# Row maxima of a two-branch attention reduced straight from PSUM, and written by one transpose and small DMAs

## The chip, the cores and the metric

One core of a Trainium2 chip runs the kernel. The metric is the device time in microseconds (us) of one execution; less is better. The core has five engines with queues of their own: TensorE (PE, matmuls), VectorE (DVE), ScalarE (ACT), GpSimd (POOL) and SyncE (SP, which only issues DMAs). Each works through its instructions in order, and waits for others by semaphores. DMAs can be issued from SP, ACT and POOL. PSUM is where matmuls write; SBUF holds everything else.

## The reference

A layer with two attentions side by side on 2048 latent tokens (a grid of 32 rows by 64 columns) and 256 context tokens, in float32. All of it is computed; the change is in how the softmax of both branches is kept from overflow.

```
# branch A: multi-head latent attention, 8 heads, 96 = 64 + 32 (rotary) dimensions
sc = einsum('bqhd,bkhd->bhqk', q, k) * scale        # 2048 queries x 2304 keys
p  = softmax(sc, axis=-1)
o  = einsum('bhqk,bkhd->bqhd', p, v)
# branch B: neighbourhood attention, 8 heads of 64, a window of 8 x 16 grid cells
s_win = einsum('bwhd,brwchd->bhwrc', qr, k_win) * scale + bias
s_ctx = einsum('bwhd,blhd->bhwl', qr, kc) * scale
p = softmax(concatenate([s_win, s_ctx], axis=-1), axis=-1)
```

Before it stand norms and one input projection, behind it gates and an output projection.

## The kernel before

The kernel runs in stages: modulation and norms (to about 200 us), the input projection (to 860), preparation for the attention (to about 1095, with the first maxima), the attention (to 2290) and the output (to 2650). Only the attention is touched.

**Branch A** is a loop over 32 units, 8 heads of 4 blocks of 512 queries. A unit has nine steps (`kp`) of 256 keys. A step computes two score tiles S (128 keys by 512 queries, three matmuls each: high and low parts of q and k), takes the exponential on ACT, adds the exponentials on POOL (`za`, L1272 and L1274) and, in bursts, multiplies them with v into `oacc` (L1224). The keys lie on the partitions of S, so the maximum of a query cannot be taken there. It is taken one unit earlier: `max_tasks(u, qh)` computes the transposed products `pm` (128 queries by up to 512 keys, L810), takes the maxima over the keys and writes their negatives into row 96 of `qh`, the high part of the next unit's queries. Row 96 of `Kh` is all ones, so the first of S's three matmuls (97 rows) subtracts the maximum.

For one tile of 128 queries the 2304 keys make five products. Two pairs of 512: the first of a pair is copied to SBUF on ACT (`msb`, L816), the second is scanned against the copy on DVE (L818), which leaves the running maximum in the last column. The rest of 256 is reduced (L823) and joined with the scan's result (L824). After four tiles, `fin` turns the four columns of `m1` into a row by four matmuls against the identity (`pmf`, L833), one row of 128 each, and ACT copies the row into `qh` (L834).

**Branch B** is a stream, `natten`, whose pieces are put between the steps of branch A by weights: `feed` hands out as many pieces as the share of steps that have passed. Per head it has 24 pieces of `n_max` for the next head (products `nm` and `nc`, reduced on DVE by L886 and L897), 24 scores `ns` (L923, L924, L940, L941) that read `KA`, `QQ`, `KBt` and `QLt`, and four pieces `fin(rb)` of `n_max`: 16 matmuls `nf` (L905) that turn the 16 columns of negated maxima into rows, and four DVE casts (L907) that write them into row 64 of `QLt`. `n_load(h)` issues the head's loads of KA, QQ, KBt, QLt, bias and v on SP's queue. It is called when the last score of the head before has been issued, and `fin` follows it.

**What sets the order.** All of it is written once in Python order and then ordered by a scheduler, which places each engine's instructions by priority and its own estimate of the time. The tasks of `max_tasks` are released by `more(frac)`: after a fraction of step `kp`, `len(tasks) * (kp + frac) / (NKP - 0.7) + 1` of them have been issued, NKP being 9. PSUM gives three buffers to `psM` and two to `psS`; `pm`, `nm`, `nc`, `ns`, S and the row matmuls take turns in these five.

Of the kernel before, what the change touches and what calls it, by code (L numbers as in the profile page):

```python
# [57 lines left out]
PB = 8  # L58
ZDVE = {1: tuple(range(1, 9))}
# [5 lines left out]
def tile_hybrid_layer(ctx: ExitStack, tc: tile.TileContext, I: dict, out: bass.AP, dbg=None):  # L65
# [81 lines left out]
    # ------------------------------------------------------------------ modulation, norms, low-rank columns  # L147
# [404 lines left out]
    # ------------------------------------------------------------------ wide columns of the in-projection  # L552
# [193 lines left out]
    # ------------------------------------------------------------------ attention  # L746
# [55 lines left out]
    def max_tasks(u, qh):  # L802
        i = (u // NB) % 2
        m1 = mq.tile([P, 4], F32, tag="m1", name=f"m1{u}")
        last = [None] * 4

        def product(qt, ci):
            a, b = ci * W, min(NK, (ci + 1) * W)
            pm = psm(f"pm{u}_{qt}_{ci}")
            nc.tensor.matmul(pm[:, :b - a], qh[0:DK, qt * P:(qt + 1) * P], Kh[i][0:DK, a:b], start=True, stop=True)  # L810
            return pm

        def pair(qt, ci):
            p0 = product(qt, ci)
            sb = mq.tile([P, W], F32, tag="msb", name=f"msb{u}_{qt}_{ci}")
            nc.scalar.activation(sb, p0, AF.Copy)  # L816
            p1 = product(qt, ci + 1)
            nc.vector.tensor_tensor_scan(sb, p1, sb, -3.0e38 if ci == 0 else last[qt], op0=ALU.max, op1=ALU.max)  # L818
            last[qt] = sb[:, W - 1:W]

        def rest(qt):
            p0 = product(qt, 4)
            nc.vector.tensor_reduce(m1[:, qt:qt + 1], p0[:, :NK - 4 * W], axis=AX.X, op=ALU.max, negate=True)  # L823
            nc.vector.scalar_tensor_tensor(out=m1[:, qt:qt + 1], in0=last[qt], scalar=-1.0, in1=m1[:, qt:qt + 1],  # L824
                                           op0=ALU.mult, op1=ALU.min)

        def fin():
            for f in zdefer:
                f()
            zdefer.clear()  # L830
            pm = psm(f"pmf{u}")
            for t in range(4):
                nc.tensor.matmul(pm[DK:DK + 1, t * P:(t + 1) * P], m1[:, t:t + 1], ident, start=True, stop=True)  # L833
            nc.scalar.activation(qh[DK:DK + 1, :], pm[DK:DK + 1, :], AF.Copy)  # L834

        o = []
        for qt in range(4):
            o += [lambda q=qt: pair(q, 0), lambda q=qt: pair(q, 2), lambda q=qt: rest(q)]
        return o + [fin]

    # neighbourhood stream
    def grid(ap):
        return ap.rearrange("p (r c) -> p r c", c=GW)
# [27 lines left out]
    def n_max(h, bn):  # L871
        mx = nv.tile([P, 2, 16], F32, tag="nmx", name=f"nmx{h}")
        m1 = nv.tile([P, 16], F32, tag="nm1", name=f"nm1{h}")
        kg = grid(NKm[:, 0:S])
# [24 lines left out]
        def fin(rb):  # L899
            if rb == 0:  # L900
                nc.vector.tensor_tensor(m1, mx[:, 0, :], mx[:, 1, :], op=ALU.max)
                nc.vector.tensor_scalar_mul(m1, m1, -1.0)
            pm = psm(f"nf{h}_{rb}")
            for cb in range(4):
                nc.tensor.matmul(pm[64:65, cb * P:(cb + 1) * P], m1[:, rb * 4 + cb:rb * 4 + cb + 1], ident,  # L905
                                 start=True, stop=True)
            nc.vector.tensor_copy(rowcol(QLt[64:65, rb * W:(rb + 1) * W]), blk(pm[64:65, :]))  # L907
# [4 lines left out]
        return o + [lambda r=r: fin(r) for r in range(4)]  # L912
# [102 lines left out]
    n_weight = 24 * WM + H * (24 * WT + 24 * WM + 4 * WM + WI)  # L1015
# [3 lines left out]
    def natten(bn, d):  # L1019
        prev = None  # L1020
        mt = n_max(0, bn)
        for f in mt[:24]:
            f()
            yield WM
        if H > 1:
            bn = n_load_max(1)
        for h in range(H):
            for i, f in enumerate(mt[24:]):
                f()
                if i == 1 and prev is not None:  # L1030
                    n_store(prev)
                    n_z(prev)
                yield WM
# [3 lines left out]
            mq_ = list(mt[:24])  # L1037
# [5 lines left out]
            for pi, pr in enumerate(npairs):  # L1043
                pts = []
                for t in pr:
                    pts.append(n_score(d, t))
                    yield WT
                    nt_ += 1
                    while mq_ and 24 - len(mq_) < nt_ * 24 / 18:
                        mq_.pop(0)()  # L1050
                        if not mq_ and h + 2 < H:
                            bn = n_load_max(h + 2)
                        yield WM
                queue.append((d, pr, pts, pi == len(npairs) - 1))
                if len(queue) > 1:
                    held.append(queue.pop(0))
                    while len(held) > HELD:
                        n_pv(*held.pop(0))
# [13 lines left out]
    # output-phase weights, prepared under the last units  # L1072
# [60 lines left out]
    # prologue  # L1133
# [100 lines left out]
    for u in range(nu):  # L1234
# [15 lines left out]
        for kp in range(NKP):  # L1250
            pt = mp.tile([P, 2, W], F32, tag="P", name=f"P{u}_{kp}", bufs=PB)
            def more(frac):
                nonlocal done
                want = min(len(tasks), int(len(tasks) * (kp + frac) / (NKP - 0.7) + 1))
# [42 lines left out]
    # ------------------------------------------------------------------ output  # L1297
# [231 lines left out]
```

## Time and profile before

| | us |
|---|---|
| three runs | 2643.67, 2647.04, 2649.07 |
| median | 2647.04 |
| span of the profiled execution | 2650.0 |
| PE busy (98% of the span) | 2588.5 |
| DVE busy (47%) | 1256.2 |
| ACT busy (39%) | 1037.3 |
| POOL busy (39%) | 1031.0 |
| mean granted clock of PE | 0.995 of 2.4 GHz |

The profiled execution has no time of its own beside its span of 2650.0 us, which is 3.0 us above the median of the three runs. Busy time is the union of an engine's records; PE's records overlap, since the next matmul begins while the one before still drains, so the cost of a matmul is read from the distance between starts and not from the length of its record.

### The profile page before, as it was taken

Reading aid. Unit: us, or ns where it says so; the run is one execution under the profiler, and the core shown is the slowest. Engines: PE = TensorE matmul, PEld = TensorE weight load, DVE = VectorE, ACT = ScalarE, POOL = GpSimd, SP = SyncE. Lnnn points to the kernel's source line nnn. Section 1 sums busy time; section 2 is a strip of 40 time slices with the busy share of each in tenths; the row PEclk is TensorE's granted clock in tenths of the full one; section 3 lists DMA queues with packets and bytes.
Section 4 is the critical chain, followed back from the end, with each engine's and each line's share of the span. In section 5 each row is a group of like instructions: output and inputs, shape, how many; then the busy total and the mean of one; then the engine's idle time right before and its main releaser. Section 6 shows DMA issues by size and latency. Waiting matters only on the chain.

```text
span 2650.0 us, 36033 instructions
## 1 busy us (share of the span) xinstructions
PE 2588.5 (98%) x13244; PEld 1861.2 (70%) x13244; DVE 1256.2 (47%) x2132; ACT 1037.3 (39%) x2030; POOL 1031.0 (39%) x797
## 2 busy tenths in 40 slices
PE   7999999999999999999999999999999999999998
PEld 4778888877799788555555656555555564798998
DVE  4663221223200310665665757574756557465564
ACT  4663332222211221455544545554545555222221
POOL 1211111112300000566665757676767686232220
PEclk9999999999999999999999999999999999999999
DMA  7536765456634465605041231414131305765552
GB/s 257 192 91 183 261 205 177 141 174 194 188 107 127 152 213 165 162 17 126 9 108 50 57 80 37 116 37 106 35 91 43 79 23 181 229 192 175 164 164 68
DMA packets 182985, 342.94 MB, mean 129 GB/s; under 512 B 25130, under 2 KB 95950, under 8 KB 175438
## 3 DMA queue, kind: packets, MB, share of 16 engines
q1 hardware_dynamic: 168872, 299.01, 38.0%
q0 software_dynamic: 13504, 41.35, 5.5%
q8 instruction: 104, 1.70, 0.3%
q14 instruction: 73, 0.60, 0.1%
q10 hardware_dynamic: 432, 0.28, 0.0%
HBM read 214.42 MB, written 126.13 MB: 129 GB/s over the span
## 4 chain that ended last, share of the span: by engine, by line
PE 87%; DVE 8%; issue 2%; DMA 1%; ACT 1%; SPq 0%; POOL 0%; DVEq 0%; ACTq 0%; POOLq 0%
PE accm L135 24%; PE S L1264 13%; PE oacc L1224 11%; PE ya L135 6%; PE pm L810 6%; PE f L135 5%; PE vacc L135 4%; DVE msb L818 3%; PE nacc L226 3%; PE no L980 3%; DVE m L824 2%; PE accf L135 2%; PE accx L135 1%; PE nf L905 1%; PE pstl L185 1%
## 5 line engine op out<-in xcount | busy, mean ns | idle before, releaser
L1274 POOL TENSOR_TENSOR za<-za,P 128x1024 f32<-128x1024 f32 x217 | 515.4, 2375 | 217.2 <-ACT P L1266 214.5
L1266 ACT ACTIVATE P<-S 128x512 f32<-128x512 f32 x576 | 340.4, 595 | 246.8 <-PE S L1264 237.2
L135 PE MATMUL accm<-hh,whi 128*128 128x512 f32 x928 | 367.0, 395 | 0.0
L135 PE MATMUL accm<-hl,whi 128*128 128x512 f32 x928 | 366.9, 395 | 0.0
L135 PE MATMUL accm<-hh,wlo 128*128 128x512 f32 x928 | 366.7, 395 | 0.0
L1224 PE MATMUL oacc<-P,V 128*64 128x512 f32 x1152 | 318.7, 615 | 0.0
L1264 PE MATMUL S<-qh,Kh 97*128 97x512 f32 x576 | 240.5, 418 | 7.7 <-DVE msb L818 3.0
L818 DVE TENSOR_TENSOR_SCAN msb<-pm,msb 128x512 f32<-128x512 f32 x128 | 155.8, 1218 | 162.8 <-ACT msb L816 137.3
L1264 PE MATMUL S<-ql,Kh 96*128 96x512 f32 x576 | 229.7, 399 | 0.0
L1264 PE MATMUL S<-qh,Kl 96*128 96x512 f32 x576 | 228.3, 396 | 0.0
L810 PE MATMUL pm<-Kh,qh 96*128 96x512 f32 (+1 forms) x640 | 215.0, 399 | 5.5 <-DVE msb L818 3.9
L816 ACT ACTIVATE msb<-pm 128x512 f32<-128x512 f32 x256 | 151.9, 594 | 167.0 <-PE pm L810 160.3
L818 DVE TENSOR_TENSOR_SCAN msb<-pm,msb,msb 128x512 f32<-128x512 f32 x128 | 163.8, 1280 | 95.5 <-ACT msb L816 93.8
L135 PEld LDWEIGHTS accm<-hh,whi 128*128 128x128 f32 x928 | 174.3, 188 | 42.6 <-issue 0.8
L135 PEld LDWEIGHTS accm<-hh,wlo 128*128 128x128 f32 x928 | 174.3, 188 | 41.9
L135 PEld LDWEIGHTS accm<-hl,whi 128*128 128x128 f32 x928 | 174.3, 188 | 41.8 <-issue 0.4
L810 PEld LDWEIGHTS pm<-Kh,qh 96*128 96x128 f32 x640 | 110.8, 188 | 116.7 <-issue 43.0
L135 PE MATMUL ya<-u,woh 128*128 128x256 f32 x1024 | 185.0, 284 | 0.2
L1224 PEld LDWEIGHTS oacc<-P,V 128*64 128x64 f32 x1152 | 73.5, 137 | 137.2 <-issue 133.9
L135 PE MATMUL f<-wfh,y 128*128 128x512 f32 (+1 forms) x528 | 162.8, 387 | 2.9 <-ACT y L1334 2.1
L824 DVE SCALAR_TENSOR_TENSOR m<-msb,m 128x1 f32<-128x1 f32 x128 | 161.5, 1262 | 2.1
L135 PEld LDWEIGHTS ya<-u,woh 128*128 128x128 f32 x1024 | 160.2, 192 | 1.4 <-DVE t L1331 0.6
(1929 smaller groups left out, 4631.6 us busy)
## 6 DMA issues: line engine op xcount, KB each, us to landing
rawc<-in_wch SPq DMA_DIRECT2D x30, 512.0 KB
KA<-kB SPq DMA_DIRECT2D x16, 576.0 KB
xl<-in_xb SPq DMA_DIRECT2D x32, 256.0 KB
wm<-in_wmodb SPq DMA_DIRECT2D x8, 1024.0 KB
kmS<-sk POOLq DMA_DIRECT2D x32, 256.0 KB, 3.8
qR<-q SPq DMA_DIRECT2D x16, 512.0 KB
qm<-sq POOLq DMA_DIRECT2D x32, 256.0 KB, 3.9
woS<-ps SPq DMA_DIRECT2D x16, 512.0 KB
```

Source lines behind the costliest of these rows:

```text
L135: nc.tensor.matmul(acc, a, b, start=(i == 0), stop=(i == n - 1))
L185: nc.tensor.matmul(pst[32 * j:32 * j + 32, :w], ones[:, 0:32], sq[:, :w], start=(kt < 4), stop=(kt >= 4))
L226: nc.tensor.matmul(acc[:, :n], a[:, k, sl], b[:, k, :n], start=(k == 0 and q == 0), stop=(k == KT - 1 and q == 2))
L810: nc.tensor.matmul(pm[:, :b - a], qh[0:DK, qt * P:(qt + 1) * P], Kh[i][0:DK, a:b], start=True, stop=True)
L816: nc.scalar.activation(sb, p0, AF.Copy)
L818: nc.vector.tensor_tensor_scan(sb, p1, sb, -3.0e38 if ci == 0 else last[qt], op0=ALU.max, op1=ALU.max)
L824: nc.vector.scalar_tensor_tensor(out=m1[:, qt:qt + 1], in0=last[qt], scalar=-1.0, in1=m1[:, qt:qt + 1], op0=ALU.mult, op1=ALU.min)
L980: nc.tensor.matmul(o_, v_, p_, start=st_, stop=last and k == n - 1, skip_group_check=True)
L1224: nc.tensor.matmul(acc[x * DV:(x + 1) * DV, :], vt[:, 2 * k + x, :], p_[:, x, :], start=(k == 0), stop=(k == NKP - 1), skip_group_check=True)
L1264: nc.tensor.matmul(sp, a[0:e, ks], b[0:e, :], start=(n == 0), stop=(n == 2))
L1266: nc.scalar.activation(pt[:, x, :], sp, AF.Exp)
L1274: ve.tensor_tensor(za, za, pt, op=ALU.add)
```

## The change

`max_tasks` has 20 tasks `part` instead of twelve: each product, of 512 or 256 keys, is reduced by DVE straight from PSUM into one of 20 columns `m5`. `fin` reduces `m5` to four negated columns, turns them by one PE transpose (128x4 to 4x128), copies that with ACT to `mr`, and writes its four rows into row 96 of `qh` by four DMAs on ACT's queue. The copies `msb`, the scans and L824 are gone. In `n_max` one reduce joins and negates both halves, one transpose (`turn`, now the 25th piece taken ahead with the other 24) gives 16 rows, ACT copies them, and `fin` writes them into row 64 of `QLt` by 16 DMAs on SP's queue. `fin` is one piece in the stream where there were four, and the stores of the head before (`n_store`, `n_z`) follow it. MLEAD is 2.0 where 0.7 stood. A few comment lines are gone as well.

```diff
+MLEAD = 2.0
 ...
     def max_tasks(u, qh):
         i = (u // NB) % 2
+        m5 = mq.tile([P, 4, 5], F32, tag="m5", name=f"m5{u}")
         m1 = mq.tile([P, 4], F32, tag="m1", name=f"m1{u}")
-        last = [None] * 4
-
-        def product(qt, ci):
+        mr = mq.tile([4, P], F32R, tag="mr", name=f"mr{u}")
+
+        def part(qt, ci):
             a, b = ci * W, min(NK, (ci + 1) * W)
             pm = psm(f"pm{u}_{qt}_{ci}")
             nc.tensor.matmul(pm[:, :b - a], qh[0:DK, qt * P:(qt + 1) * P], Kh[i][0:DK, a:b], start=True, stop=True)
-            return pm
-
-        def pair(qt, ci):
-            p0 = product(qt, ci)
-            sb = mq.tile([P, W], F32, tag="msb", name=f"msb{u}_{qt}_{ci}")
-            nc.scalar.activation(sb, p0, AF.Copy)
-            p1 = product(qt, ci + 1)
-            nc.vector.tensor_tensor_scan(sb, p1, sb, -3.0e38 if ci == 0 else last[qt], op0=ALU.max, op1=ALU.max)
-            last[qt] = sb[:, W - 1:W]
-
-        def rest(qt):
-            p0 = product(qt, 4)
-            nc.vector.tensor_reduce(m1[:, qt:qt + 1], p0[:, :NK - 4 * W], axis=AX.X, op=ALU.max, negate=True)
-            nc.vector.scalar_tensor_tensor(out=m1[:, qt:qt + 1], in0=last[qt], scalar=-1.0, in1=m1[:, qt:qt + 1],
-                                           op0=ALU.mult, op1=ALU.min)
+            nc.vector.reduce_max(m5[:, qt, ci:ci + 1], pm[:, :b - a], axis=AX.X)
 ...
             zdefer.clear()
+            nc.vector.tensor_reduce(m1, m5, axis=AX.X, op=ALU.max, negate=True)
             pm = psm(f"pmf{u}")
+            nc.tensor.transpose(pm[0:4, 0:P], m1, ident)
+            nc.scalar.activation(mr, pm[0:4, 0:P], AF.Copy)
             for t in range(4):
-                nc.tensor.matmul(pm[DK:DK + 1, t * P:(t + 1) * P], m1[:, t:t + 1], ident, start=True, stop=True)
-            nc.scalar.activation(qh[DK:DK + 1, :], pm[DK:DK + 1, :], AF.Copy)
+                nc.scalar.dma_start(bc(qh[DK:DK + 1, t * P:(t + 1) * P]), bc(mr[t:t + 1, :]))
 ...
-        def fin(rb):
-            if rb == 0:
-                nc.vector.tensor_tensor(m1, mx[:, 0, :], mx[:, 1, :], op=ALU.max)
-                nc.vector.tensor_scalar_mul(m1, m1, -1.0)
-            pm = psm(f"nf{h}_{rb}")
-            for cb in range(4):
-                nc.tensor.matmul(pm[64:65, cb * P:(cb + 1) * P], m1[:, rb * 4 + cb:rb * 4 + cb + 1], ident,
-                                 start=True, stop=True)
-            nc.vector.tensor_copy(rowcol(QLt[64:65, rb * W:(rb + 1) * W]), blk(pm[64:65, :]))
+        def turn():
+            nc.vector.tensor_reduce(m1, mx.rearrange("p t q -> p q t"), axis=AX.X, op=ALU.max, negate=True)
+            pm = psm(f"nf{h}")
+            nc.tensor.transpose(pm[0:16, 0:P], m1, ident)
+            nc.scalar.activation(mr, pm[0:16, 0:P], AF.Copy)
+
+        def fin():
+            for qb in range(16):
+                rb, cb = divmod(qb, 4)
+                nc.sync.dma_start(grid(bc(QLt[64:65, :]))[:, rb * 8:rb * 8 + 8, cb * 16:cb * 16 + 16],
+                                  bc(mr[qb:qb + 1, :]).rearrange("o (r c) -> o r c", r=8))
 ...
-    n_weight = 24 * WM + H * (24 * WT + 24 * WM + 4 * WM + WI)
+    n_weight = 25 * WM + H * (24 * WT + 25 * WM + WM + WI)
 ...
-            for i, f in enumerate(mt[24:]):
+            for i, f in enumerate(mt[25:]):
                 f()
-                if i == 1 and prev is not None:
+                if prev is not None:
 ...
-                want = min(len(tasks), int(len(tasks) * (kp + frac) / (NKP - 0.7) + 1))
+                want = min(len(tasks), int(len(tasks) * (kp + frac) / (NKP - MLEAD) + 1))
```

How the change moves instructions is shown at three places. The first is PE at the end of unit 13, where unit 14's maxima are finished. `pm14_3_4` is the last product of unit 14, `S13_8_1` the second score tile of unit 13's last step, `zp12` belongs to unit 12's sums, `ns3` and `nc4` to the heads 3 and 4 of branch B; the last column is the output's shape, and the number at the end of a name only tells buffers apart. Before:

```order
L810 MATMUL pm14_3_4_12868<-Kh1_8343,qh14_12288 128x256
L895 MATMUL nc4_4_12873<-NKm_8336,NQs_8337 128x256 x2
L1264 MATMUL S13_8_0_12878<-qh13_11953,Kh1_8343 128x512
L1264 MATMUL S13_8_0_12878<-ql13_12339,Kh1_8343 128x512
L1264 MATMUL S13_8_0_12878<-qh13_11953,Kl1_8345 128x512
L1180 MATMUL zp12_12883<-za12_12292,ones_68 32x128 x4
L833 MATMUL pmf14_12891<-ident_63,m114_12606 1x128 x3
L940 MATMUL ns3_('w', 3, 1)_12897<-QQ_8341,KA_8339 128x352
L833 MATMUL pmf14_12891<-ident_63,m114_12606 1x128
L941 MATMUL ns3_('w', 3, 1)_12897<-QLt_8338,KBt_8340 128x352
L1264 MATMUL S13_8_1_12904<-qh13_11953,Kh1_8343 128x512
L1264 MATMUL S13_8_1_12904<-ql13_12339,Kh1_8343 128x512
```

After, with lines 10 lower:

```order
L812 MATMUL pm14_3_4_12719<-Kh1_8343,qh14_12174 128x256
L1254 MATMUL S13_7_0_12723<-qh13_11847,Kh1_8343 128x512
L1254 MATMUL S13_7_0_12723<-ql13_12221,Kh1_8343 128x512
L1254 MATMUL S13_7_0_12723<-qh13_11847,Kl1_8345 128x512
L1170 MATMUL zp12_12728<-za12_12180,ones_68 32x128 x4
L821 MATMUL pmf14_12737<-ident_63,m114_12487 4x128
L883 MATMUL nc4_4_12744<-NKm_8336,NQs_8337 128x256 x2
L1254 MATMUL S13_7_1_12748<-qh13_11847,Kh1_8343 128x512
L1254 MATMUL S13_7_1_12748<-ql13_12221,Kh1_8343 128x512
L1254 MATMUL S13_7_1_12748<-qh13_11847,Kl1_8345 128x512
L871 MATMUL nm4_10_12754<-NKm_8336,NQs_8337 128x480
L930 MATMUL ns3_('w', 3, 1)_12758<-QQ_8341,KA_8339 128x352
```

Before, the first score of unit 14, `S14_0_0`, follows this piece after the rest of `S13_8_1`, two pairs of `oacc`, two `no` and one `nm`. Now the single transpose stands ahead of `S13_7_1`, and up to `S14_0_0` come the rest of `ns3`, the two tiles of step 8, two pairs of `oacc` and one `nm`.

The second place is ACT, the same end of unit 13. `P13_7` and `P13_8` are exponentials of steps 7 and 8. Before:

```order
L1266 ACTIVATE P13_7_12850<-S13_7_1_12863 128x512
L944 ACTIVATE np3_('w', 0, 1)_12857<-np3_('w', 0, 1)_12857 128x384
L1266 ACTIVATE P13_8_12877<-S13_8_0_12878 128x512
L1183 ACTIVATE zs12_12888<-zp12_12883 128x128
L834 ACTIVATE qh14_12288<-pmf14_12891 1x512
L944 ACTIVATE np3_('w', 3, 1)_12898<-np3_('w', 3, 1)_12898 128x352
L1266 ACTIVATE P13_8_12877<-S13_8_1_12904 128x512
```

After, where the four rows of `mr14` go to `qh14` by DMA:

```order
L1256 ACTIVATE P13_7_12722<-S13_7_0_12723 128x512
L1173 ACTIVATE zs12_12733<-zp12_12728 128x128
L822 ACTIVATE mr14_12488<-pmf14_12737 4x128
L824 DMA qh14_12174<-mr14_12488 1x16x8 x4
L1256 ACTIVATE P13_7_12722<-S13_7_1_12748 128x512
L934 ACTIVATE np3_('w', 3, 1)_12759<-np3_('w', 3, 1)_12759 128x352
L1256 ACTIVATE P13_8_12765<-S13_8_0_12766 128x512
```

One copy has become one smaller copy and four DMA issues, which stand a step earlier, ahead of the exponential of `S13_7_1`.

The third place is SP's queue at head 1, where its loads are issued. Before:

```order
L792 DMA V_10663<-vaS 128x1152
L857 DMA KA<-kB_119 64x2304
L858 DMA KA<-kB_119 64x2304
L859 DMA QQ<-qR_123 64x2048
L860 DMA QQ<-qR_123 64x2048
L861 DMA KBt<-kB_119 64x2304
L862 DMA QLt<-qR_123 64x2048
L864 DMA bt_9969<-in_biasT 128x480
L1193 DMA zmS_106<-zs_9992 4x128
```

After, with ten rows of `nmr` (the sixteen turned maxima) ahead of the loads and six behind them:

```order
L896 DMA QLt<-nmr_8903 1x8x16 x10
L793 DMA V_10596<-vaS 128x1152
L844 DMA KA<-kB_119 64x2304
L845 DMA KA<-kB_119 64x2304
L1183 DMA zmS_106<-zs_9914 4x128
L846 DMA QQ<-qR_123 64x2048
L847 DMA QQ<-qR_123 64x2048
L848 DMA KBt<-kB_119 64x2304
L849 DMA QLt<-qR_123 64x2048
L851 DMA bt_9945<-in_biasT 128x480
L777 DMA qh_9963<-qm_77 96x512
L896 DMA QLt<-nmr_8903 1x8x16 x6
```

The loads stand in the same order; what is new are the sixteen small DMAs around them.

## Rows read from the trace of the kernel before

**Rows 1.** Busy us (records) by engine in the attention, granted clock, DMA share, GB/s:

```profile
860.00:2260.00 1400.00, 1364.18 (x6505) 840.73 (x6504) 783.94 (x1101) 659.88 (x1198) 794.92 (x445) 0.99 0.34 90
```

**Rows 2.** PE's waits, 860 to 2290 us: us in total, times, longest:

```profile
PE pmf L833 <- DVE m L824: 14.8, 17, 3.4
PE pm L810 <- DVE msb L818: 3.9, 14, 0.4
PE S L1264 <- DVE msb L818: 3.0, 9, 0.6
```

**Rows 3.** Groups of PE by form, 860 to 2290 us: records, busy us, mean ns:

```profile
L833 PE MATMUL pmf<-ident,m 128*1 128x128 f32 x256 | 36.6, 273 | 15.0 <-DVE m L824 14.8
L905 PE MATMUL nf<-ident,nm 128*1 128x128 f32 x256 | 32.5, 272 | 0.0
```

**Rows 4.** Timeline of PE from 1113 us: start, duration, line, operation, records:

```profile
1113.10 1.03 PE L905 MATMUL nf<-ident,nm 128*1 128x128 f32 x8
1114.07 0.50 PE L1264 MATMUL S<-qh,Kh 97*128 97x512 f32 x1
...
1114.96 1.03 PE L905 MATMUL nf<-ident,nm 128*1 128x128 f32 x8
1115.93 1.07 PE L1224 MATMUL oacc<-P,V 128*64 128x512 f32 x2
1116.93 0.51 PE L810 MATMUL pm<-Kh,qh 96*128 96x512 f32 x1
```

**Rows 5.** Groups of DVE by form in the attention:

```profile
L818 DVE TENSOR_TENSOR_SCAN msb<-pm,msb,msb 128x512 f32<-128x512 f32 x128 | 163.8, 1280 | 95.5 <-ACT msb L816 93.8 <-PE ns_('w', 2, 2)_13301 L941 0.3
L824 DVE SCALAR_TENSOR_TENSOR m<-msb,m 128x1 f32<-128x1 f32 x128 | 161.5, 1262 | 2.1
L818 DVE TENSOR_TENSOR_SCAN msb<-pm,msb 128x512 f32<-128x512 f32 x128 | 155.8, 1218 | 162.8 <-ACT msb L816 137.3 <-PE S L1264 20.3 <-PE pm L810 4.4
L823 DVE TENSOR_REDUCE m<-pm 128x1 f32<-128x256 f32 x128 | 53.2, 415 | 23.8 <-PE pm L810 22.4
L897 DVE TENSOR_REDUCE nmx<-nc 128x2 f32<-128x512 f32 x64 | 43.6, 682 | 41.5 <-PE nc L895 41.5
```

**Rows 6.** Timeline of all engines at the end of unit 13:

```profile
1604.63 2.35 POOL L1274 TENSOR_TENSOR za<-za,P 128x1024 f32<-128x1024 f32 x1 [1.78 <-ACT P L1266]
...
1605.29 1.71 DVE L824 SCALAR_TENSOR_TENSOR m<-msb,m 128x1 f32<-128x1 f32 x1
...
1607.06 0.38 PE L833 MATMUL pmf<-ident,m 128*1 128x128 f32 x2 [0.42 <-DVE m L824]
...
1607.47 0.59 ACT L834 ACTIVATE qh<-pmf 1x512 fp32r<-1x512 f32 x1 [1.34 <-PE pmf L833]
...
1611.49 0.40 PE L1264 MATMUL S<-qh,Kh 97*128 97x512 f32 x1
```

**Rows 7.** Groups of ACT by form in the attention:

```profile
L816 ACT ACTIVATE msb<-pm 128x512 f32<-128x512 f32 x256 | 151.9, 594 | 167.0 <-PE pm L810 160.3 <-DVE msb L818 6.0
...
L1183 ACT ACTIVATE zs<-zp 128x128 f32<-128x128 f32 x30 | 8.2, 272 | 0.8 <-PE zp L1180 0.8
```

**Rows 8.** The tile zmS, a 2 KB DMA per unit: issue to landing:

```profile
DMA to landing us min/median/max: 1.9/2.0/2.0
```

**Rows 9.** Timeline of SP's queue at head 1: start, duration of the issue:

```profile
1228.42 0.45 SPq L857 DMA_DIRECT2D KA<-kB  x1
1228.91 0.59 SPq L858 DMA_DIRECT2D KA<-kB  x1
...
1231.46 0.59 SPq L862 DMA_DIRECT2D QLt<-qR  x1
```

**Rows 10.** Timeline of PE at head 1:

```profile
1228.23 0.33 PE L941 MATMUL ns_('w', 2, 3)_9867<-QLt,KBt 113*128 113x360 f32 x1
...
1258.12 0.40 PE L923 MATMUL ns_('c', 0, 0)_10104<-QQ,KA 128*128 128x512 f32 x1
```

**Rows 11.** Busy us and DMA in the window of head 1's loads:

```profile
1228.00:1258.00 30.00, 30.00 (x177) 17.14 (x177) 12.95 (x18) 14.19 (x26) 17.29 (x9) 1.00 0.68 156
```

More of the change, by code (lines that the diff above doesn't have):

```diff
@@ L830, in fin @@
             zdefer.clear()
+            nc.vector.tensor_reduce(m1, m5, axis=AX.X, op=ALU.max, negate=True)
             pm = psm(f"pmf{u}")
+            nc.tensor.transpose(pm[0:4, 0:P], m1, ident)
+            nc.scalar.activation(mr, pm[0:4, 0:P], AF.Copy)
             for t in range(4):
-                nc.tensor.matmul(pm[DK:DK + 1, t * P:(t + 1) * P], m1[:, t:t + 1], ident, start=True, stop=True)
-            nc.scalar.activation(qh[DK:DK + 1, :], pm[DK:DK + 1, :], AF.Copy)
[L836 to L839, printed above, removed]
+                nc.scalar.dma_start(bc(qh[DK:DK + 1, t * P:(t + 1) * P]), bc(mr[t:t + 1, :]))
+        return [lambda q=qt, c=ci: part(q, c) for qt in range(4) for ci in range(5)] + [fin]
     def grid(ap):
@@ L873, in n_max @@
         m1 = nv.tile([P, 16], F32, tag="nm1", name=f"nm1{h}")
+        mr = nv.tile([16, P], F32R, tag="nmr", name=f"nmr{h}")
         kg = grid(NKm[:, 0:S])
@@ L911, in n_max @@
             o += [lambda q=2 * b2: win(q), lambda q=2 * b2 + 1: win(q), lambda b=b2: cmax(b)]
-        return o + [lambda r=r: fin(r) for r in range(4)]
+        return o + [turn, fin]
     def n_score(d, t):
@@ L1021, in natten @@
         mt = n_max(0, bn)
-        for f in mt[:24]:
+        for f in mt[:25]:
             f()
@@ L1036, in natten @@
                 mt = n_max(h + 1, bn)
-            mq_ = list(mt[:24])
+            mq_ = list(mt[:25])
             d["za"] = nv.tile([P, S], F32, tag="nza", name=f"nza{h}")
@@ L1048, in natten @@
                     nt_ += 1
-                    while mq_ and 24 - len(mq_) < nt_ * 24 / 18:
+                    while mq_ and 25 - len(mq_) < nt_ * 25 / 18:
                         mq_.pop(0)()
```

## The prediction

> **What bounds the kernel now.** First the table of stretches, to see which engine is full where the change acts. In the attention (860 to 2260 us) PE is busy 1364.18 of 1400 us at a granted clock of 0.99 of 2.4 GHz; DVE has 783.94, ACT 659.88 and POOL 794.92 [rows 1]. So PE is the bound: a matmul taken away there is worth its whole time, a DVE or ACT instruction is worth only the PE wait that it causes, and 35.8 us of PE idle is all that waits can give. The second view is PE's list of waits. Its three largest entries are the row matmuls pmf behind L824 (14.8 us in 17 waits), the products pm behind the scan L818 (3.9) and the scores S behind the same scan (3.0), 21.7 us together [rows 2]. All three go back to the chain that the change replaces. No load stands in that list.
>
> **Removed: row matmuls on PE.** Each record of pmf and nf reads 272 or 273 ns and there are 256 of each [rows 3], but records overlap, so I take a spacing. Eight nf records are four matmuls (two records for one fp32 matmul): they begin at 1113.10 and the next matmul at 1114.07, 0.97 us, so one costs 0.2425 us [rows 4]. Before there are 32x4 pmf and 8x16 nf matmuls; after, one transpose of the same 128 moving columns per unit and per head. 32x3 + 8x15 = 216 matmuls go: 216 x 0.2425 = **52.4 us**, on the path. Nothing hides it: at the row matmuls PE is the busy engine. The transpose has four or sixteen stationary columns where a row matmul has one, a form that no row shows. If it took twice the 0.2425, the 40 would cost 10 us more; if nothing, 10 us less. I take 0.2425, the row with the same moving operand.
>
> **Replaced: the maxima.** For one query tile DVE now does 1.218 (scan), 1.280 (scan), 0.415 (reduce of 256) and 1.262 (L824, on one element a row), 4.2 us, 16.7 us per unit [rows 5]. After: sixteen reduces of 512 from PSUM at 0.682 (the reduce L897 reads the same shape) and four at 0.415 make 12.6 us, and a last reduce of 4x5 numbers. That last one has no row. At least it costs the accumulator read of about 0.1, at most the 1.262 of L824; I take 0.4 us, near L823. DVE is under no pressure either way: four us per unit less is worth nothing by itself. On ACT 256 copies of 0.594 us (151.9) and the copies L834 go [rows 7]; ACT was not the bound, so this is worth nothing by itself either.
>
> What it can give is PE's waits. L824 is the case: its shortest work is tiny, yet it takes 1.262 on the mean. At the end of unit 13 it starts at 1605.29 and ends at 1607.00, and the POOL addition that started at 1604.63 ends at 1606.98; PE then starts the last pmf at 1607.06 after a wait of 0.42 us [rows 6]. The two-input DVE instruction ends when the POOL one does. The Trainium skill ("SBUF — State Buffer", section "Who interferes with whom") says that a DVE instruction with two SBUF inputs contends with a GpSimd instruction that reads SBUF, and that `tensor_reduce` on trn2 never contends; the row on L824 agrees with the first half, and no row of before shows the second, a reduce from SBUF beside POOL. By that rule the new last reduce is never held; without it the sum would carry up to 1.3 us per unit at this place, the rival "the waits stay". With no copy before the scan, a product is free for reuse after one reduce instead of ACT and then a scan, so the waits of pm and S should go too. The transpose still waits for the last pm, its reduce (0.415) and the small reduce; between the last pm and pmf the order above shows one S score (three matmuls) and the zp matmuls, about 1.2 us. I let 18 of the 21.7 us go and keep about 4.
>
> **Added: the row by DMA, per unit.** Before, ACT writes row 96 of qh straight from PSUM: at unit 13's end from 1607.47 for 0.59 us, and S of unit 14 starts at 1611.49, 3.4 us after it [rows 6]. After, the way is: ACT copy of 4x128 (nearest row zs, 272 ns [rows 7]), four DMA issues on ACT's queue, and a landing. An issue is priced by SP's of 0.45 to 0.59 us [rows 9], since no row shows one on ACT beside activations; a 2 KB transfer of the same kind, zmS, lands 1.9 to 2.0 us after its issue [rows 8]. With about 0.3 for the two handovers: 0.3 + 0.27 + 4x0.52 + 2.0 = 4.65 us; at least 4.4 and, with ACT busy in an exponential of 0.6, 5.3. The cover is PE's work between pmf and S. MLEAD 2.0 sets fin one step earlier, so that three scores of three matmuls, two pairs of oacc and six smaller matmuls stand there at unit 14. A score takes 0.89 (1114.07 to 1114.96) and a pair 1.00 (1115.93 to 1116.93) [rows 4]; the small ones, with 256 to 480 columns, some 0.15 to 0.2 each: 2.7 + 2.0 + 1.1 = 5.8 us, 5.0 where scores follow each other closely. So it is mostly hidden, narrowly: cover less chain lies between -0.3 and 1.4 at a typical unit, and a few units have a score less between. I charge 0.5 us to each of 32 units, **+16**; the ends are 0 and 1.5 (0 to 48). Behind the four issues on ACT stand the exponentials of the next score tile; they come 2 us later and are needed only two steps on, by oacc, so I add nothing.
>
> The Trainium skill ("DMA: Bandwidth & Descriptors", "Rules for kernel authors") speaks against this: many small transfers should be coalesced into one, and under 64 KB one pays mostly overhead, of which the page's fixed part is about 2.0 us per DMA. The 1.9 to 2.0 of zmS agrees [rows 8]; if these fixed parts ran one after another instead of overlapped, the time would be that of the first rival.
>
> **Added: QLt's row, per head.** Sixteen DMAs stand on SP's queue: ten ahead of the loads of KA, QQ, KBt and QLt and six behind them (order above). The ten wait for the last read of the old QLt, as KA waits for the last read of KA. Head 1 before: last read 1228.23, KA issued 1228.42, QLt 1231.46, first score of the head 1258.12 [rows 9, 10]. That is 29.6 us in which 3.5 MB must land, while the core moves 156 GB/s on the mean at a DMA share of 0.68 [rows 11]; at full share that is 156/0.68 = 229 GB/s, 15 us, at the mean rate 22. After, the sixteen nf matmuls and two of the stream's four steps are gone from this window, and counted by the spacings the first score comes 19 to 21 us after the last read and the first read of QLt 24 to 28 us. KA now leaves 10x0.52 = 5 us later. KA and QQ (2.2 MB, 9.5 to 14 us) then land at about 17 to 21 us, all four with KBt and QLt at 22 to 29. Cover and need are about equal; the stall lies between 0 and 7 us. I take 2 us for each of 7 heads, **+14**. SP itself is mostly idle, so its other issues lose nothing.
>
> **Sum** against the profiled execution, 2650.0 us: 2650.0 - 52.4 - 18 + 16 + 14 = 2609.6. The median of the runs is 2647.04, 3.0 less, so the forecast is **2607 us**.
>
> **Rivals.** (1) **The row chain outlasts its cover.** If the four landings come one after another, the chain is 0.57 + 4x2.0 = 8.6 against a cover of 5.4: 3.2 us per unit, 32 x 3.2 = 102 in place of 16, 2693 us, slower than before. It decides from (2655 - 2593.6)/32 = 1.9 us per unit. Against it: the issues do not wait for one another's data. For: the cover is narrow. (2) **The head's loads come late.** 7 us for each of 7 heads, 49 in place of 14: 2642, no change. For it: the shorter window and five us of row DMAs ahead of KA. Against: the share of 0.68 shows room. (3) **The waits stay.** The last reduce comes behind others in DVE's order or is held like L824: 18 us are not saved, 2625. (4) **All covers hold.** No stall at units and heads and no wait left: 2650 - 52.4 - 21.7 - 3 = 2573. (5) The change does not do what it says: not so, since the 216 matmuls, the copies and the scans are gone from the built order.
>
> **Chances.** Forecast 0.48, (3) 0.18, (4) 0.15, (1) 0.10, (2) 0.09. About 0.2% (5.3 us) is what a measurement of this kernel can tell from no change. Faster by more than that: the forecast, (3), (4) and a third of (2), 0.84; within: 0.06, the rest of (2); slower: 0.10, (1). The range leaves out (1) and little of (4)'s lower end: 2572 to 2645.
>
> **What would show it.** Right: PE's records of pmf and nf fall from 512 to 80, the spacing of a transpose is 0.24; PE's list has no wait on L824 or a scan, and the last reduce takes well under 1.26; S of a new unit waits for the DMA of qh by under 1 us, ns of a new head for KA or QLt by a few. Wrong: an entry "S behind DMA qh" of 60 us or more (1), "ns behind DMA" of 50 (2), "pmf behind DVE" at 15 again (3), or a PE idle in the attention that has grown though no wait names a DMA, which I have no term for.

## The result and the profile after

| | before | after |
|---|---|---|
| median of the runs, us | 2648.06 | 2661.64 |
| range, us | 2643.67 to 2649.47 | 2653.05 to 2666.67 |
| span of the profiled execution, us | 2650.0 | 2651.2 |

The ratio after/before is 1.0054, with a 95% interval of 1.0037 to 1.0071. The change makes the kernel slower by half a per cent, where 1.5% faster was forecast. The profiled execution of after is the fastest of its four, so its trace shows some 9 us less loss than the median has.

The table of stretches, for the attention, against [rows 1]:

```profile
860.00:2260.00 1400.00, 1363.62 (x6011) 818.85 (x6010) 617.01 (x1218) 504.41 (x948) 794.35 (x445) 0.98 0.34 90
```

DVE lost 167 us and ACT 155, as the edit says. PE lost 494 records and is as busy as before: 1363.62 against 1364.18 us. That is the riddle. PE's groups, 860 to 2350 us, after:

```profile
L1214 PE MATMUL oacc<-P,V 128*64 128x512 f32 x1152 | 364.9, 620 | 1.6 <-ACT P L1256 1.5
...
L821 PE MATMUL pmf<-ident,m 128*4 128x128 f32 x32 | 8.7, 271 | 0.0
L890 PE MATMUL nf<-ident,nm 128*16 128x128 f32 x8 | 2.2, 275 | 0.0
```

and of before, the row that the prediction did not look at:

```profile
L1224 PE MATMUL oacc<-P,V 128*64 128x512 f32 x1152 | 318.7, 615 | 0.0
```

The row matmuls went from 36.6 + 32.5 [rows 3] to 8.7 + 2.2 us. But the product with v, of which no line was touched, has the same 1152 records of nearly the same length, and its busy time (the union of its records) rose by 46 us. Records of equal length with a longer union overlap less. PE's waits, 860 to 2290 us, against [rows 2]:

```profile
PE S L1254 <- DMA qh<-mr: 17.9, 9, 6.5
PE S L1254 <- DMA QLt<-nmr: 3.1, 1, 3.1
PE S L1254 <- DVE m L813: 3.0, 4, 1.7
PE S L1254 <- ACT P L1256: 2.7, 5, 1.4
```

The 21.7 us of [rows 2] are gone, and about as much has come in their place, now behind small DMAs. The second line belongs to the first. S does not read QLt, and the wait is that of a unit's first S for its row:

```profile
1948.13 2.44 ACTq L824 DMA_DIRECT2D qh<-mr  x4
...
1956.10 0.51 PE L1254 MATMUL S<-qh,Kh 97*128 97x512 f32 x1 [3.12 <-DMA QLt<-nmr]
```

The semaphores that this S waits for are those of the four DMAs of qh, the last of which reports at 1955.96; the DMAs of QLt that begin at 1954.89 use the same ones, and so the list names QLt. PE waits 21.0 us for qh's row, in ten units, and nowhere for QLt.

**Where PE's time is.** For the tables below each matmul is counted from its start to the next one's start (or to its own end, where PE then idles), over the whole span; a stretch at the granted clock of 1.2 GHz counts half, and its other half is booked as "clock". The sums stay 12 us under the spans, 5 before the first matmul and 7 behind the last.

| us | before | after | difference |
|---|---|---|---|
| row matmuls or transposes (pmf, nf) | 61.0 | 1.5 | -59.5 |
| products with v (oacc and no) | 372.7 | 425.8 | +53.1 |
| all other matmuls | 2143.0 | 2136.0 | -7.0 |
| clock | 11.5 | 25.4 | +13.9 |
| idle | 49.4 | 50.2 | +0.8 |

The saving on PE is there, and larger than forecast. It was given back by two terms that the sum did not have: the products with v, and the clock.

**What happened to the products with v.** A step's product is two matmuls of 64 columns, one for each half of `oacc`'s partitions. PE's timeline in before (start, duration, records; two records are one matmul):

```profile
1499.80 1.94 PE L1224 MATMUL oacc<-P,V 128*64 128x512 f32 x8
1501.57 0.33 PE L980 MATMUL no<-np_('w', 0, 3)_11878,nv 128*64 128x192 f32 x1
```

and in after:

```profile
1547.34 1.07 PE L1214 MATMUL oacc<-P,V 128*64 128x512 f32 x2
1548.34 0.43 PE L871 MATMUL nm<-NKm,NQs 112*128 112x352 f32 x1
...
1549.40 1.08 PE L1214 MATMUL oacc<-P,V 128*64 128x512 f32 x4
1550.41 0.50 PE L913 MATMUL ns_('c', 2, 0)_12320<-QQ,KA 128*128 128x512 f32 x1
1550.84 1.07 PE L1214 MATMUL oacc<-P,V 128*64 128x512 f32 x2
1551.84 0.50 PE L1254 MATMUL S<-qh,Kh 97*128 97x512 f32 x1
```

Two steps in a row, four matmuls, take 1.77 us. A pair by itself takes 1.01 us, and half a pair by itself 1.00: the two halves run at the same time when they are neighbours, and a half that stands alone takes as long as the pair. Here PE's order is: the first half of step 2, then an `nm`, an `ns` and two `pm`, the second half of step 2 beside the first of step 3, another `ns`, the second half of step 3. So 3.0 us went into what takes 1.77. In the built order 74 halves of oacc stand alone before, 156 after.

### The profile page after: what moved, and what is told of

The parts are those of the page before. It is cut to its first block, busy times and chain, and to the rows that moved or that the text cites. A ratio compares the mean times of both kernels' runs of the same rounds, so it can differ in the third digit from the quotient of the medians.

```text
span 2651.2 us, 35036 instructions
## 1 busy us (share of the span) xinstructions
PE 2589.1 (98%) x12772; PEld 1841.0 (69%) x12772; DVE 1088.7 (41%) x2252; ACT 883.2 (33%) x1782; POOL 1032.7 (39%) x797
## 4 chain that ended last, share of the span: by engine, by line
PE 88%; DMA 4%; DVE 3%; ACT 1%; ACTq 1%; issue 1%; POOL 1%; SPq 1%; POOLq 0%; DVEq 0%
PE accm L136 25%; PE S L1254 15%; PE oacc L1214 11%; PE pm L812 6%; PE ya L136 5%; PE f L136 4%; PE vacc L136 4%; PE no L970 3%; PE nacc L227 3%; DMA qh<-mr 2%; PE accf L136 2%; PE accx L136 1%; ACTq L824 1%; PE pstl L186 1%; PE nm L871 1%
## 5 line engine op out<-in xcount | busy, mean ns | idle before, releaser
L813 DVE TENSOR_REDUCE m<-pm 128x1 f32<-128x512 f32 (+1 forms) x640 | 388.2, 632 | 548.0 <-PE pm L812 542.8
L1214 PE MATMUL oacc<-P,V 128*64 128x512 f32 x1152 | 364.9, 620 | 1.6 <-ACT P L1256 1.5
L812 PE MATMUL pm<-Kh,qh 96*128 96x512 f32 (+1 forms) x640 | 227.8, 401 | 3.9 <-DVE m L813 1.8
L812 PEld LDWEIGHTS pm<-Kh,qh 96*128 96x128 f32 x640 | 120.9, 190 | 122.9 <-issue 64.7
L1214 PEld LDWEIGHTS oacc<-P,V 128*64 128x64 f32 x1152 | 81.5, 137 | 151.5 <-issue 136.5
L1254 PEld LDWEIGHTS S<-qh,Kh 97*128 97x128 f32 x576 | 110.5, 192 | 102.8 <-issue 37.9
L136 PE MATMUL ya<-u,wol 128*128 128x256 f32 x512 | 144.9, 283 | 0.0
L357 ACT ACTIVATE g<-accm 128x512 f32<-128x512 f32 x88 | 52.2, 593 | 253.3 <-PE accm L136 213.4
```

The lines of the kernel that those rows point to most:

```text
L136: nc.tensor.matmul(acc, a, b, start=(i == 0), stop=(i == n - 1))
L357: nc.scalar.activation(s1, acc, AF.Sigmoid)
L813: nc.vector.reduce_max(m5[:, qt, ci:ci + 1], pm[:, :b - a], axis=AX.X)
L1214: nc.tensor.matmul(acc[x * DV:(x + 1) * DV, :], vt[:, 2 * k + x, :], p_[:, x, :], start=(k == 0), stop=(k == NKP - 1), skip_group_check=True)
L1254: nc.tensor.matmul(sp, a[0:e, ks], b[0:e, :], start=(n == 0), stop=(n == 2))
```

## Experiments

Theory A: the torn halves carry the loss. Theory B: the new way of the row carries it, by ACT's issues, by landings behind the heads' loads, and by the lower clock after such waits.

**Keep the halves together.** In `pv`, and in the same manner in `n_pv`, for the kernel after (e1) and before (e2):

```diff
+GLUE = 400
 ...
-                for x in range(2):
-                    nc.tensor.matmul(acc[x * DV:(x + 1) * DV, :], vt[:, 2 * k + x, :], p_[:, x, :],
-                                     start=(k == 0), stop=(k == NKP - 1), skip_group_check=True)
+                a0 = nc.tensor.matmul(acc[0:DV, :], vt[:, 2 * k, :], p_[:, 0, :],
+                                      start=(k == 0), stop=(k == NKP - 1), skip_group_check=True)
+                with tc.high_priority(offset=GLUE), tc.issue_after(a0.ins):
+                    nc.tensor.matmul(acc[DV:P, :], vt[:, 2 * k + 1, :], p_[:, 1, :],
+                                     start=(k == 0), stop=(k == NKP - 1), skip_group_check=True)
```

> The kernel after, with the two halves of each product with v kept next to each other on PE (the second half gets a higher priority and is queued behind the first); nothing else. In the built order the halves of oacc that stand alone fall from 156 to 20. Theory A (the 60 us of row matmuls were saved, and given back because the new order tears the halves apart, so that each runs alone): oacc and no lose 45 to 55 us against the kernel after, time about 2605 us. Theory B (given back by the DMA of the rows: PE waits at S and the lower granted clock after them): the waits and the clock stay, time 2650 to 2660 us.

> The kernel before with the same edit: halves of oacc that stand alone fall from 74 to 0. Theory A: 37 pairs at 0.7 to 1 us, 25 to 35 us less, time 2612 to 2622 us; with the halves together in both, the change itself should then be worth 10 to 25 us. Theory B: no more than 10 us less, time about 2640 us.

Measured: e1 2631.98 us (0.9947 of before, interval 0.9927 to 0.9967), e2 2621.18 us (0.9906, 0.9886 to 0.9926). Theory A hit e2 and missed e1, and theory B missed both: in e1 the products with v fall by 39 us to 387, idle and clock rise by 16. Torn halves cost 23 us in before and 39 in after, but with the halves together in both, the change itself is still 11 us slower than without it. Theory A explains a good part and not all.

**Take the change apart.** e8 is before with `(NKP - 2.0)` for `(NKP - 0.7)` in `more`, nothing else. e3 is after with the old `fin` of both branches put back (row matmuls, ACT copy, DVE casts, the old weights), so that the reduces from PSUM and MLEAD are left:

```diff
-            nc.tensor.transpose(pm[0:4, 0:P], m1, ident)
-            nc.scalar.activation(mr, pm[0:4, 0:P], AF.Copy)
             for t in range(4):
-                nc.scalar.dma_start(bc(qh[DK:DK + 1, t * P:(t + 1) * P]), bc(mr[t:t + 1, :]))
+                nc.tensor.matmul(pm[DK:DK + 1, t * P:(t + 1) * P], m1[:, t:t + 1], ident, start=True, stop=True)
+            nc.scalar.activation(qh[DK:DK + 1, :], pm[DK:DK + 1, :], AF.Copy)
```

> The kernel before with only the release of the max tasks changed (NKP - 2.0 for NKP - 0.7): fin falls one step earlier, nothing else. Lone halves of oacc go from 74 to 120. Theory A: 23 torn pairs at 0.5 to 0.7 us, 10 to 20 us slower than before, 2656 to 2666 us, less what an earlier fin takes off the 15 us of waits at pmf. Theory B: no DMA, so no loss; 2635 to 2646 us.

> The kernel after with the old way of writing the rows in both branches (four pmf and sixteen nf matmuls, one ACT copy, four DVE casts), so only the reduces from PSUM and MLEAD are left of the change. No small DMA is left; 126 halves of oacc stand alone. Theory A: row matmuls back to 60 us, the 126 lone halves cost some 20 us more than before, the waits on the scan (about 20 us) gone: 2640 to 2655 us. Theory B: no DMA waits, no lower clock, waits on the scan gone: 2620 to 2630 us.

Measured: e8 2674.09 us (1.0099, 1.0072 to 1.0126), e3 2627.37 us (0.9923, 0.9905 to 0.9942). With after this is a chain of three edits, each measured:

| us | before | + MLEAD (e8) | + reduces (e3) | + rows by DMA (after) |
|---|---|---|---|---|
| median | 2648 | 2674 | 2627 | 2662 |
| halves of oacc alone, built order | 74 | 120 | 126 | 156 |
| row matmuls or transposes | 61.0 | 58.9 | 59.2 | 1.5 |
| products with v | 372.7 | 397.5 | 400.6 | 425.8 |
| all other matmuls | 2143.0 | 2141.5 | 2126.8 | 2136.0 |
| clock | 11.5 | 14.6 | 3.1 | 25.4 |
| idle | 49.4 | 47.3 | 19.1 | 50.2 |

MLEAD alone costs 26 us, nearly all of it in the products with v (24.8 by the table); that is more than theory A had priced. Its oacc and pmf groups:

```profile
L1224 PE MATMUL oacc<-P,V 128*64 128x512 f32 x1152 | 347.6, 620 | 2.5 <-DVE or L1231 2.5
...
L833 PE MATMUL pmf<-ident,m 128*1 128x128 f32 x256 | 33.6, 272 | 0.5 <-DVE m L824 0.5
```

The idle before pmf fell from 15.0 to 0.5 us, and PE's waits for the scan at pm rose from 3.9 to 16.0, so the earlier release moves a wait and tears the order. The reduces are worth 47 us by the medians; the table has 28 less of idle, 15 of other matmuls and 11 of clock, and 3 more of products with v. The rows by DMA save 58 us of matmuls and cost 88: 25 in the products with v, 22 in clock, 31 in idle, 9 in other matmuls. That is 30 us slower by the profiled executions, 34 by the medians. e3 is where theory B put it and 13 us under theory A; for e8 theory A had the direction, theory B had no loss. So the last step is mostly theory B's, but for the 25 us in the products with v, and the first is theory A's.

**ACT's issues.** In after, with `nc.sync.dma_start` for `nc.scalar.dma_start` at qh's row (e4), and the same with the halves together (e6):

> The kernel after with the four DMAs of qh's row issued on SP's queue instead of ACT's; 132 halves of oacc stand alone instead of 156. Theory A: about 10 us less than after, 2650 us. Theory B, in the form that ACT's 2.4 to 2.8 us of issuing per unit holds back the exponentials: 25 us or more less, under 2637 us; in the form that the landing itself comes late: within 5 us of after.

> The kernel after with qh's rows issued on SP, and the halves kept together: 18 lone halves instead of 132. Theory A: oacc and no fall from 406 to about 365 us, 2560 to 2570 us. Theory B: within 10 us of the 2604 that rows on SP gave.

Measured: e4 2604.5 us (0.9834, 0.9813 to 0.9855), 57 us under after; e6 2585.38 us (0.9771, 0.9747 to 0.9795). e4's time is that of theory B in the form that has ACT held. Its profiled execution, the slowest of four, is 44 us under after's, the fastest of four: by the table the products with v lose 20 us, clock 10, idle 7, other matmuls 7. e1 and e6 are the closest pair, with 20 and 18 lone halves: the same DMAs, issued from ACT or from SP, differ by 47 us. In after's timeline at head 2 one sees a way in which the issues cost PE time:

```profile
1392.13 0.27 ACT L822 ACTIVATE mr<-pmf 4x128 fp32r<-4x128 f32 x1 [1.10 <-PE pmf L821]
...
1392.43 2.43 ACTq L824 DMA_DIRECT2D qh<-mr  x4
...
1393.27 0.50 PE L1254 MATMUL S<-qh,Kh 97*128 97x512 f32 x1
...
1394.96 0.60 ACT L1256 ACTIVATE P<-S 128x512 f32<-128x512 f32 x1 [2.56 <-DMA qh<-mr]
...
1395.61 0.50 PE L1254 MATMUL S<-qh,Kh 97*128 97x512 f32 x1 [1.37 <-ACT P L1256]
```

Four issues hold ACT 2.43 us. The exponential behind them waits 2.56 us, and PE waits 1.37 us for it, since S needs the PSUM buffer that the exponential frees. On SP no exponential stands behind the issues. But this way is a small part of the 47 us. By the table e6 has 15 less than e1 in the products with v, 14 in clock, 12 in idle and 4 in other matmuls. PE's waits behind the exponentials P fall only from 7.5 to 3.7 us. Those for qh's row, in e1 (first) and in e6, are fewer:

```profile
PE S L1261 <- DMA qh<-mr: 27.2, 13, 6.6
```

```profile
PE S L1261 <- DMA qh<-mr: 20.1, 3, 12.4
```

Why the clock and the products with v follow the issuing queue no run separates; the order of the instructions moved with it. e6 is 19 us under e4, half of what theory A expected and more than theory B did: by the table the products with v fall by 34 us (406.0 to 371.9), and idle and clock take 7 back. e4 and e6 both have one wait of 12.4 us at S for qh's DMA, at the start of a unit near the end of the attention, where SP issues loads for the output.

**The landing.** At head 1 of after, ACT's queue and PE:

```profile
1229.01 2.69 ACTq L824 DMA_DIRECT2D qh<-mr  x4
...
1240.06 0.77 PE L1254 MATMUL S<-qh,Kh 97*128 97x512 f32 x1 [6.49 <-DMA qh<-mr]
```

and the table of stretches there, and in a unit's end without loads (DMA share and GB/s last):

```profile
1226.00:1241.00 15.00, 8.52 (x58) 5.20 (x55) 0.60 (x2) 3.39 (x7) 8.03 (x4) 0.84 0.87 185
...
1265.00:1280.00 15.00, 14.54 (x50) 6.97 (x51) 6.06 (x15) 5.05 (x9) 12.55 (x7) 1.00 0.00 1
```

From the end of the last issue (1231.70) to S are 8.4 us, where zmS [rows 8] landed in 2.0. The head's loads stand before the row: SP issued QQ and KBt in the same microseconds, and the share is 0.87. Of the ten waits on qh, four of the five longest (1240, 1531, 1956, 2185) lie in stretches of 14 or 15 us with a share of 0.72 to 0.92, the fifth (1917) at 0.56. The Trainium skill ("DMA: Bandwidth & Descriptors", section "Issuing engines are not separate DMA queues") says that DMAs of all issuing engines run on the same 16 DMA engines and interleave; the 8.4 us agree.

**The two branches apart.** e7 is after with the old row of qh only, e9 with the old nf only and qh's row on SP; the halves are together in both. e5, the reference for both, has the old rows in both branches (e3 with the halves together):

> The kernel of reduces only (old rows by matmuls in both branches, no small DMA), with the halves of each product with v kept together: 4 lone halves of oacc instead of 126. Theory A (torn halves carry the loss): oacc and no together fall from 401 us to about 350, as they did to 349 in the kernel before with the same edit; 2575 to 2585 us. Theory B (the DMA way of the row carries it, torn halves are a side effect): there is no DMA here, so no more than 10 us under the 2627 of reduces only.

> The kernel after with qh's row written the old way (four pmf matmuls and one ACT copy), QLt's row still by one transpose and 16 DMAs on SP, and the halves kept together. It tells the two branches apart. If the head's 16 DMAs cost nothing, it stands 29 us (the nf matmuls) under reduces only with halves together, about 2550 us. If they hold back the head's loads, as the prediction charged (14 us, at most 49), it stands 15 us under it or even above it, 2560 to 2600 us.

> QLt's row the old way (nf matmuls, no DMA by heads), qh's row by one transpose and four DMAs on SP, halves kept together. The other half of the split that the old row of qh with halves together made. If S waits for qh's DMA only where it stands behind a head's DMAs on SP's queue, the 12.4 us wait near 2146 of rows on SP is gone and PE's S-behind-DMA is under 8 us in all: 2555 to 2565 us, since the pmf matmuls (31 us) are gone against reduces only with halves together (2583). If the small DMAs land late behind the loads of the heads, wherever they are issued, the wait stays at 15 us or more: 2570 to 2585 us.

Measured: e5 2582.81 us (0.9756, 0.9733 to 0.9779), e7 2594.51 (0.9811, 0.9782 to 0.984), e9 2569.12 (0.9705, 0.969 to 0.9719). e5 is where theory A put it, 45 us under e3, nearly all of it in the products with v. QLt's row by DMA is 12 us slower than the sixteen matmuls it replaces, though it takes 28 us off PE; qh's row by DMA from SP is 14 us faster. e9 stands between its two expectations: the long wait shrank to 9.8 us and did not go, so it does not come from the heads' small DMAs on SP's queue:

```profile
PE S L1258 <- DMA qh<-mr: 16.1, 4, 9.8
```

What QLt's DMAs cost is not a wait of PE for QLt. At head 2 of e7 (timeline of all engines):

```profile
1358.46 16.64 SPq L895 DMA_DIRECT2D QLt<-nmr  x11
...
1367.42 0.50 PE L912 MATMUL ns_('c', 0, 0)_11133<-QQ,KA 128*128 128x512 f32 x1
...
1373.38 0.50 PE L912 MATMUL ns_('c', 2, 0)_11186<-QQ,KA 128*128 128x512 f32 x1
...
1376.53 0.50 PE L1259 MATMUL S<-qh,Kh 97*128 97x512 f32 x1 [0.75 <-ACT P L1261]
...
1378.19 0.50 PE L1259 MATMUL S<-qh,Kh 97*128 97x512 f32 x1 [0.69 <-ACT P L1261]
...
1384.13 0.63 PE L913 MATMUL ns_('c', 0, 0)_11133<-QLt,KBt 113*128 113x512 f32 x1
```

The eleven row DMAs behind the loads take 16.6 us to issue, 9.9 of them the first. Two context scores have their first matmul and wait with the second until QLt is whole, 16.7 us for the first; they hold two of the five PSUM buffers, and S, left with three, waits for ACT. Head 2 is the longest case: at every head of e7 the first two or three context scores stand open in this way, 3 to 17 us, where e5 has three in all, 2 to 5 us. e11 puts the matmul of QLt first:

```diff
-            nc.tensor.matmul(ps, KA[:, ks], QQ[:, qs_], start=True, stop=False)
-            nc.tensor.matmul(ps, KBt[:, ks], QLt[:, qs_], start=False, stop=True)
+            nc.tensor.matmul(ps, KBt[:, ks], QLt[:, qs_], start=True, stop=False)
+            nc.tensor.matmul(ps, KA[:, ks], QQ[:, qs_], start=False, stop=True)
```

> The old row of qh with halves together (2595 us), and in the neighbourhood's context scores the matmul of KBt and QLt first, that of KA and QQ second. As it was, the first scores of a head open two of the five PSUM buffers with KA and QQ and hold them 11 to 17 us until QLt's small DMAs have landed; S waits for ACT's exponentials in the rest. If that holding is what QLt's DMAs cost, its waits of S and pm behind ACT (5 us) and half of its lone no products go: 2575 to 2585 us. If the DMAs hold up the loads themselves, nothing changes: 2590 to 2600 us, with PE waiting for QLt.

Measured: 2586.74 us (0.9771, 0.9756 to 0.9785), 8 us under e7, whose interval it just touches, and just above what was expected. PE's wait at S behind ACT fell from 3.9 us (e7, first) to 0.7 and idle by 7; a wait for QLt appeared, in the open now:

```profile
PE S L1259 <- ACT P L1261: 3.9, 7, 0.7
```

```profile
PE ns_('c', 0, 0)_11133 L912 <- DMA QLt<-nmr: 2.4, 1, 2.4
```

So the holding is about 8 of the some 40 us that QLt's DMAs cost (12 net, 28 saved). The products with v stand 15 us above e5 in e7, and 18 in e11; why the halves of the heads' first products run alone there was not tried, and stays open.

**Does the earlier release matter with the halves together?** e10 is e5 with MLEAD 0.7:

> Reduces only with halves together, and the release of the max tasks as before (0.7 in place of 2.0): 2 lone halves of oacc. If the earlier fin is what took away the waits at pmf, they come back: 8 to 15 us slower than the 2583 of reduces only with halves together, 2591 to 2598 us. If the reduces alone took them away (no scan, no two-input DVE instruction at the end), it is within 6 us of it; with the halves together MLEAD should then not matter.

Measured: 2577.67 us (0.9732, 0.9715 to 0.9748), 5 us under e5; the intervals overlap. The reduces alone took the waits at pmf away, and with the old rows MLEAD 2.0 is worth nothing once the halves are held together. It costs some 5 us there, where e8 had 26, which bears out that e8 pays for torn halves; e8 itself with the halves together was not run, nor e9 or e12 with MLEAD 0.7.

**The fastest.** e12 is e9 with the old row of qh where it had waited:

```diff
+            if u < 2 or u >= 29:
+                for t in range(4):
+                    nc.tensor.matmul(pm[DK:DK + 1, t * P:(t + 1) * P], m1[:, t:t + 1], ident, start=True, stop=True)
+                nc.scalar.activation(qh[DK:DK + 1, :], pm[DK:DK + 1, :], AF.Copy)
+                return
             nc.tensor.transpose(pm[0:4, 0:P], m1, ident)
```

> The fastest so far (QLt's row the old way, qh's row by DMAs on SP, halves together, 2569 us), with the old row of qh in units 0, 1 and 29 to 31, where S had waited 4.2, 9.8 and 1.3 us for qh's DMAs: at unit 1 behind head 0's loads, at the end behind the output's loads on SP's queue. If those waits stood for the place of the DMA alone, they go (15 us) against five times three row matmuls (3.6 us): about 2557 us, with PE's S-behind-DMA under 2 us. If they only move to another unit, it stays within 4 us of 2569.

Measured: 2557.19 us, 0.9656 of before (0.964 to 0.9672), 92 us faster than before and 104 than after. Its waits for qh's row:

```profile
PE S L1263 <- DMA qh<-mr: 1.6, 1, 1.6
```

The waits stood for the place of the DMA and did not move to another unit.

## Why the prediction was wrong

**What held.** PE is the bound, and the row matmuls' time there is gone: 52.4 us were forecast and 59.5 measured. The difference is mostly the 40 transposes, charged at 0.2425 us each. They have one record each (40 records, not the 80 expected) and cost 1.5 us in all. That such time is worth its whole length is shown by e12 against e5: 24 us less of row matmuls by the table, 26 us less by the medians. The waits on the scan and on L824 are gone, and the last reduce takes 0.17 us where 0.4 was taken (DVE's line, shortest, median and longest in ns):

```profile
L819 DVE TENSOR_REDUCE m<-m x32: 159/173/175, 870.4 to 2246.2; 128x4 f32<-128x20 f32 x32
```

It is never held, though POOL's additions go on beside it; L824 took 1.262 on the mean in [rows 5]. The Trainium skill ("SBUF — State Buffer", "Who interferes with whom") says so of `tensor_reduce`, and these 159 to 175 ns agree. That half of the change is right: e3 with reduces and MLEAD beats before by 18 us, and e5 and e10, where the halves are together too, by 63 and 71, against the 25 of e2 with the halves together alone.

**The step that failed first.** "MLEAD 2.0 sets fin one step earlier" was used for the cover it gives, and was charged nothing. The order was read for where pmf and S stand and not for what the move does to the neighbours of everything else. e8 prices it at 26 us, 25 of them in the products with v. The new rows tear more halves, for another 25 us of the same kind (e3 against after). The forecast took the cost of every untouched matmul as that of before; for a matmul that shares PE with its neighbour, cost is a property of the order.

**The second.** "Behind the four issues on ACT stand the exponentials of the next score tile; they come 2 us later and are needed only two steps on, by oacc, so I add nothing." The exponential is not only needed by oacc: it frees a PSUM buffer for a later S, and S is on PE's path. The four issues take 2.4 to 2.7 us where they are shown, not 2.1. Moving them off ACT gives 47 us (e1 against e6), 57 without the halves together. That the issues on ACT are not free is shown; of the 47, PE's waits behind the exponentials are about 4 and those for qh's row 7, and how the clock (14) and the products with v (15) come to the rest stays open.

**The third**, with the mechanism right and the place wrong, is the landing. The row chain was charged 16 us at 0.5 us in each unit; the traced wait is 21.0 us, in ten units. zmS landed in 2.0 us; behind a head's loads qh's row took 8.4. That the price came out near is luck. The rival of the row chain expected a wait in every unit, 102 us, and did not come.

**The fourth**, the head: 14 us were charged for PE waiting on loads or QLt. PE waits for neither in after. (The six loads of KA, QQ, KBt and QLt are 3.3 MB by the shapes in the order, not 3.5, which changes little.) What QLt's row costs (12 us net in e7 against e5, some 40 with the 28 saved) is idle of other kinds and products with v; about 8 us of it come by two held PSUM buffers, which no term had.

**The clock** had no term either. Before, 0.99 was read as full speed. In and after the wait of 6.49 us that ends at 1240, the table of stretches shows PE of after at the lower level of 1.2 GHz (PEclk 0.51 of 2.4 GHz):

```profile
1236.00:1246.00 10.00, 5.94 (x16) 2.79 (x20) 0.69 (x1) 1.79 (x3) 2.50 (x2) 0.51 0.86 186
```

The same stretch in before, with PE busy for all 10 us, has 1.00:

```profile
1236.00:1246.00 10.00, 10.00 (x70) 5.89 (x71) 3.09 (x4) 5.26 (x9) 6.40 (x4) 1.00 1.00 209
```

All nine stretches at 1.2 GHz in the attention of after begin during a wait of PE or within 2 us behind one, and so do the four of before. Not every wait is followed by one: a wait of 2.9 us near 2060 in before is not. The link is read from the times alone; no run tries it. By it a wait can cost more than its length: the clock takes 14 us more in after than in before, 22 more than in e3.

## What to carry to other kernels

When a change moves instructions, price the order and not only the instructions: look for groups that are cheap only because they are neighbours, and compare how often they are whole in both built orders. A DMA issue holds ACT as long as an exponential of 128x512 does (0.6 us), so it belongs on a queue behind which nobody stands, and its landing time has to be read from a stretch with the same loads in flight. A tile of PSUM that is opened before its last operand has landed takes a buffer from everyone else; put the matmul with the late operand first.

## What the runs showed of the hardware that was not expected

Two matmuls of 64 columns that write different halves of the partitions run at the same time if they stand next to each other: 1.01 us for the pair, 1.00 for one alone, 1.77 for two pairs. A DMA of 512 bytes from SBUF to SBUF takes about 0.6 us to issue on ACT (median 0.60 in after) or SP (0.58 in e4), as much as one of 576 KB (0.45 to 0.59 in [rows 9]); one of QLt's on SP took 9.9 us in e7. A reduce of 20 columns from SBUF took 0.17 us beside POOL's additions, where a two-input instruction on one column had taken 1.26.
